# Seven block products for eight in seven W_up pairs of layer 1 of an encoder

## The chip, the core and the metric

The kernel runs on one core of one Trainium2 chip. The metric is the device time of one execution in microseconds (us), smaller is better. Five things work side by side on a core: TensorE (PE, matmuls, with its weight loads as PEld), VectorE (DVE), ScalarE (ACT), GpSimd (POOL) and SyncE (SP), which issues the DMAs. Each runs its own instructions in a fixed order; one that waits holds up all that stand behind it on its engine.

## What is computed

Two layers of an encoder over 512 positions of 1024 channels. The part that matters here is the second half of each layer:

```python
h = rmsnorm(x, norm2[l])
up = dwconv_centred(h @ w_up[l], conv_w[l], conv_b[l])   # 1024 -> 2 x 2816, then 3 taps along positions
gate, val = up[..., :D_FF], up[..., D_FF:]
x = x + (jax.nn.silu(gate) * val) @ w_down[l]            # 2816 -> 1024
```

Ahead of it each layer has a projection, a Fourier group, windowed attention and the output projection W_o, which the change does not touch.

## The kernel before

All activations are held transposed: channels on the 128 partitions, the 512 positions along the free axis. x is eight tiles x0 to x7 of 128x512, and h2[k] is the normed tile k, split into a high and a low part.

A product in float32 is made of three matmuls in fp32r (mm3): high by high (L120), low weights by high (L121), high weights by low (L122). So each weight has to be split: wsplit casts the high part on ACT (whi, L90) and subtracts for the low part on DVE (wlo, L93). whi and wlo have 5 buffers each of 512 columns; the raw weights (wraw) have 3 of 1024.

A pair fi of the FFN is a gate tile (column tile fi of W_up) and a value tile (fi + 22). There are 22 pairs in two halves (HALVES) of 11, each followed by its share of W_down. For each tile of a pair:

- one load of 512 KB on SP, two whi and two wlo (wchunks);
- 8 x 3 matmuls 128x512 into one bank of the rota FFN_BANKS;
- u, the bank times rb2 (the row factor of the norm, which is ready only after W_up has begun), on DVE (L93);
- the convolution: ACT with scale and bias into y, then two scalar-tensor-tensors on DVE, in place (L96).

Behind both tiles come Silu on ACT, the gate multiply (on POOL in layer 1, L93 POOL, on DVE in layer 0) and the split of the result into gu (ACT high, DVE low), which W_down reads. While layer 0 runs its FFN, weights of layer 1's first part are split ahead (presplit, `ahead`); in layer 1 nothing is.

PSUM has eight banks: three mm, two sc, two tp, one av. The tp banks serve transposes and the sums of the norms, and stand idle in the FFN of layer 1. A scheduler orders each engine's instructions by its own estimate of when they can start; the program's order is only where it begins, so instructions of neighbouring pairs are mixed on DVE and ACT.

## Time and profile before

| | |
|---|---|
| runs | 1056.22, 1057.18, 1057.36 us (median 1057.18) |
| the profiled execution | 1056.14 us |
| its span in the trace | 1054.3 us |
| mean granted TensorE clock | 0.999 |
| layer 1's W_up, first half | about 715 to 824 us of the span |

A row of the timeline gives the start and the length in us, the engine, the line, the operation and its tiles, a count where several follow one another, and in brackets the idle time ahead of it and what ended that. A row of a group gives busy us and the mean in ns of one, then the idle time ahead.

### The profile page before, as it was taken

The page shows a single profiled execution, that of the slowest core. Times are in us where ns is not written, and L with a number is a line of the kernel's source. Part 1 is how long each engine was busy: PE and PEld are TensorE (multiplying, and loading weights), DVE is VectorE, ACT ScalarE, POOL GpSimd, SP SyncE. Part 2 cuts the span into 40 slices and gives each one's busy share as a digit, 9 for nine tenths or more (in the row PEclk, how much of TensorE's full clock was granted, in tenths as well). Part 3 has the DMA queues.
Part 4 walks back from the last instruction along what each step waited for, and adds up shares of the span by engine and source line. Part 5 has one row for each costly group of instructions (what it writes and reads, how often), then busy time and mean ns, then how long its engine had stood idle before and what let it go on. Part 6 is the DMA issues. An engine that isn't in the chain of part 4 may idle for free.

```text
span 1054.3 us, 14425 instructions
## 1 busy us (share of the span) xinstructions
PE 1038.2 (98%) x5107; PEld 873.2 (83%) x5107; DVE 726.8 (69%) x1384; ACT 507.9 (48%) x939; POOL 90.8 (9%) x164
## 2 busy tenths in 40 slices
PE   8998999999999999999999999999999999999998
PEld 8986778888888888888899887888888888888887
DVE  8878768697767777777519775478877336878632
ACT  5339755455444445455423785246554224454421
POOL 0004410000000000000000152001101000101100
PEclk9999999999999999999999999999999999999999
DMA  7232152332269833239856313333332333332241
GB/s 273 83 115 87 58 193 81 100 100 96 78 226 353 324 100 101 89 114 322 280 181 221 113 62 99 122 100 94 101 101 74 96 115 100 98 101 82 82 150 48
DMA packets 60475, 140.03 MB, mean 133 GB/s; under 512 B 6642, under 2 KB 22258, under 8 KB 60404
## 3 DMA queue, kind: packets, MB, share of 16 engines
q1 hardware_dynamic: 60404, 139.12, 40.5%
q8 instruction: 40, 0.66, 0.3%
q14 instruction: 31, 0.25, 0.1%
HBM read 116.02 MB, written 23.07 MB: 132 GB/s over the span
## 4 chain that ended last, share of the span: by engine, by line
PE 93%; DVE 2%; DMA 2%; ACT 1%; issue 1%; POOL 0%; SPq 0%; ACTq 0%; DVEq 0%; POOLq 0%
PE ps L122 28%; PE ps L120 28%; PE ps L121 28%; PE ps L118 3%; PE ps L548 2%; PE ps L541 2%; PE ps L529 1%; DMA wraw<-in_w_qkv_dram 1%; PE ps L234 1%; PE ps L227 1%; ACT tA L90 0%; DMA x<-in_xT_dram 0%; DVE tA L533 0%; ACT act L90 0%; PE ps L500 0%
## 5 line engine op out<-in xcount | busy, mean ns | idle before, releaser
L90 ACT ACTIVATE whi<-wraw 128x512 fp32r<-128x512 f32 (+1 forms) x296 | 182.0, 616 | 290.8 <-PE ps L122 278.4
L120 PE MATMUL ps<-act,whi 128*128 128x512 f32 x768 | 298.9, 390 | 0.0
L121 PE MATMUL ps<-act,wlo 128*128 128x512 f32 x768 | 298.3, 389 | 0.0
L122 PE MATMUL ps<-act,whi 128*128 128x512 f32 x768 | 298.2, 389 | 0.0
L93 DVE TENSOR_TENSOR wlo<-wraw,whi 128x512 fp32r<-128x512 f32 (+1 forms) x304 | 219.7, 726 | 103.4 <-ACT whi L90 102.0
L122 PEld LDWEIGHTS ps<-act,whi 128*128 128x128 f32 x768 | 144.2, 188 | 30.1
L120 PEld LDWEIGHTS ps<-act,whi 128*128 128x128 f32 x768 | 144.2, 188 | 29.7
L121 PEld LDWEIGHTS ps<-act,wlo 128*128 128x128 f32 x768 | 144.2, 188 | 29.7
L96 DVE SCALAR_TENSOR_TENSOR tF<-tF,pb,tF 128x511 f32<-128x511 f32 x176 | 133.5, 763 | 11.1 <-ACT tF L90 8.7
L93 DVE TENSOR_TENSOR tF<-ps,rb 128x512 f32<-128x512 f32 x104 | 71.2, 689 | 77.9 <-PE ps L122 64.7
L120 PE MATMUL ps<-slab,whi 128*128 128x512 f32 (+2 forms) x212 | 82.2, 388 | 0.0
L122 PE MATMUL ps<-slab,whi 128*128 128x512 f32 (+2 forms) x212 | 79.9, 380 | 0.4 <-DVE slab L93 0.3
L121 PE MATMUL ps<-slab,wlo 128*128 128x512 f32 (+2 forms) x212 | 80.0, 378 | 0.0
L90 ACT ACTIVATE tF<-tF,pb 128x512 f32<-128x512 f32 x88 | 71.7, 816 | 11.3 <-DVE tF L93 4.6
L93 DVE TENSOR_TENSOR x<-x,ps 128x512 f32<-128x512 f32 (+1 forms) x49 | 32.9, 674 | 36.5 <-PE ps L122 36.3
L93 POOL TENSOR_TENSOR tF<-tF,tF 128x512 f32<-128x512 f32 x22 | 30.2, 1371 | 256.1 <-DVE tF L96 224.1
L120 PE MATMUL ps<-pT,whi 128*128 128x512 f32 (+1 forms) x132 | 50.5, 383 | 0.0
L121 PE MATMUL ps<-pT,wlo 128*128 128x512 f32 (+1 forms) x132 | 50.5, 383 | 0.0
L122 PE MATMUL ps<-pT,whi 128*128 128x512 f32 (+1 forms) x132 | 50.5, 383 | 0.0
L538 POOL TENSOR_SCALAR tA<-tA,den 128x256 f32<-128x256 f32 (+1 forms) x64 | 37.4, 590 | 145.1 <-DVE den L537 144.6
L533 DVE CUSTOM_DVE_ANT_0 tA<-ps,pb,nsink 128x256 f32<-128x256 f32 (+1 forms) x64 | 37.8, 603 | 14.5 <-PE ps L529 9.7
L122 PEld LDWEIGHTS ps<-slab,whi 128*128 128x128 f32 x212 | 39.7, 188 | 8.3 <-DVE slab L93 0.9
(178 smaller groups left out, 1485.0 us busy)
## 6 DMA issues: line engine op xcount, KB each, us to landing
wraw<-in_w_up_dram SPq DMA_DIRECT2D x88, 512.0 KB, 3.5
wraw<-in_w_down_dram SPq DMA_DIRECT2D x32, 512.0 KB, 3.7
kept<-tA SPq DMA_DIRECT2D x56, 256.0 KB, 5.7
whi<-kept SPq DMA_DIRECT2D x28, 256.0 KB, 3.0
wlo<-kept SPq DMA_DIRECT2D x28, 256.0 KB, 3.0
kept<-tA SPq DMA_DIRECT2D x32, 192.0 KB, 4.4
wraw<-in_w_down_dram SPq DMA_DIRECT2D x32, 192.0 KB, 2.4
wraw<-in_w_o_dram SPq DMA_DIRECT2D x8, 512.0 KB, 3.7
```

What stands on the lines that cost most here:

```text
L90: return nc.scalar.activation(out, in_, func, **kw)
L93: return (eng or nc.vector).tensor_tensor(out, a, b, op=op)
L96: return nc.vector.scalar_tensor_tensor(out=out, in0=a, scalar=s, in1=b, op0=op0, op1=op1)
L118: nc.tensor.matmul(out, a[0], b[0], start=start, stop=stop, **kw)
L120: nc.tensor.matmul(out, a[0], b[0], start=start, stop=False, **kw)
L121: nc.tensor.matmul(out, a[1], b[0], start=False, stop=False, **kw)
L122: nc.tensor.matmul(out, a[0], b[1], start=False, stop=stop, **kw)
L227: nc.tensor.matmul(pt[:, 2 * b:2 * b + 2], acc[:, b * P:(b + 1) * P], ones2, start=True, stop=True)
L533: nc.vector.tensor_tensor_reduce(out=pr[:, :n], in0=sc[:, :n], in1=mask[:, m0:m0 + n], scale=qs_scale[p][:, i, e:e + 1], scalar=nsink[:, l ...
L538: nc.gpsimd.tensor_scalar(pr[:, :n], pr[:, :n], den[:, i:i + 1], 1.0, op0=ALU.mult, op1=ALU.mult)
L541: tr = nc.tensor.transpose(pp[:, j * P:(j + 1) * P], pr[:, j * P:(j + 1) * P], ident)
L548: pv = nc.tensor.matmul(py[64 * e:64 * e + 64, i0 * P:(i1 + 1) * P], vp[:, j, 64 * g:64 * g + 64], pT[:, half, e, b0:b0 + 2 * (i1 - i0) + ...
```

## The change

In layer 1, the pairs 6, 8, 12, 14, 16, 18 and 20 are computed another way (up_seven); below they are the seven pairs, the others the eight pairs. The pair's two column tiles and the eight tiles of h are taken as a product of 2 x 2 blocks: a11 and a12 are the gate tile's weights for channels 0 to 511 and 512 to 1023, a21 and a22 the value tile's, and h is cut likewise into channels and into positions 0 to 255 and 256 to 511. Eight block products become seven, each of 4 x 3 matmuls 128x256, with sums of weights (s1 to s4, on DVE: s3 and s2 in a tile of their own, s1 in a21's place, s4 in a12's) and sums of h (T1 to T4). X and Y gather in the two tp banks, Z in a bank of the rota. X is copied by ACT after a11's product, goes on gathering, and is read three times more.

The sums of h are made once, by seven_h, behind each of the pairs 0 to 3: two ACT scalings, four half-wide DVE operations and two splits, into places that are free by then (h_rooms). And the gate multiply of layer 1 is on DVE now for all 22 pairs. The convolution is the same code in a function of its own; `pace`, and `acc` for layer 1, hold nothing that an instruction comes from.

```diff
--- before.py
+++ after.py
@@ -34,6 +34,8 @@
 FFN_BANKS = ("mm", "mm", "mm", "av", "sc", "sc")
 HALVES = [(0, 11), (11, 11)]
 
+SEVEN = ((), (6, 8, 12, 14, 16, 18, 20))
+
 def encoder_kernel(tc, t):
 
@@ -145,6 +147,8 @@
         return [wsplit(raw[:, c:min(c + step, n)], eng) for c in range(0, n, step)]
 
     kept = {}
+
+    pace = [None]
 
     def presplit(l):
 
@@ -371,6 +375,106 @@
         nc.sync.dma_start(raw.rearrange("p (k c) -> p k c", k=2),
                           t["w_in"][l, 2 * kk * P:2 * (kk + 1) * P, 0:FW].rearrange("(k p) c -> p k c", p=P))
         return [raw[:, k * 512:(k + 1) * 512] for k in range(2)]
+
+    LO, HI = slice(0, 256), slice(256, 512)
+
+    def sums_of_b(b1, b2):
+        t13, t24 = temp(512, "tF"), temp(512, "tF")
+        tt(t13[:, LO], b1[:, HI], b1[:, LO], ALU.subtract)
+        tt(t13[:, HI], b2[:, HI], b1[:, HI], ALU.subtract)
+        tt(t24[:, LO], t13[:, LO], b2[:, HI], ALU.subtract)
+        tt(t24[:, HI], t24[:, LO], b2[:, LO], ALU.add)
+        return t13, t24
+
+    def parts(g, src, keys, room):
+        two = [next(room), next(room)]
+        split(*two, src)
+        for key, cols in zip(keys, (LO, HI)):
+            g[key] = [z[:, cols] for z in two]
+
+    def h_rooms(l):
+
+        for tag in ("th0", "th1", "tl0", "tl1", "wt0", "wt1", "v", "accA", "accF", "acc"):
+            yield cp.tile([P, 512], F32R, tag=tag, name=nm("room"), bufs=1)
+        yield cp.tile([P, 512], F32R, tag="rb", name=nm("room"), bufs=2)
+        for _ in range(2):
+            yield tp.tile([P, 516], F32R, tag="tail", name=nm("room"), bufs=2)[:, :512]
+        for _ in range(2):
+            yield temp(512, "sq", F32R)
+        yield cp.tile([P, 512], F32R, tag="room", name=nm("room"), bufs=1)
+
+    def seven_h(k, l, h2, room):
+
+        b = [temp(512, "tF") for _ in range(2)]
+        for i in range(2):
+            act(b[i], x[k + 4 * i], scale=g2[:, l, k + 4 * i:k + 4 * i + 1])
+        g = dict(B11=[z[:, LO] for z in halves(h2[k])], B21=[z[:, LO] for z in halves(h2[k + 4])],
+                 B22=[z[:, HI] for z in halves(h2[k + 4])])
+        t13, t24 = sums_of_b(*b)
+        parts(g, t13, ("T1", "T3"), room)
+        parts(g, t24, ("T2", "T4"), room)
+        return g
+
+    def up_eight(l, fi, h2, ts, rb2):
+        for z in range(2):
+            w = wchunks(t["w_up"][l, fi + z * FT], 1024)
+            nps[0] += 1
+            o = psum(FFN_BANKS[nps[0] % len(FFN_BANKS)])
+            for k in range(KT):
+                mm3(o, [q[:, (k % 4) * P:(k % 4 + 1) * P] for q in w[k // 4]], [h2[k][:, s, :] for s in range(2)],
+                    k == 0, k == KT - 1)
+            u = temp(512, "tF")
+            tt(u, o, rb2, ALU.mult)
+            yield u
+
+    def up_seven(l, fi, h2, ts, rb2):
+        a, b = [wload(t["w_up"][l, fi + z * FT], 1024) for z in range(2)]
+        a11, a12, a21, a22 = a[:, :512], a[:, 512:], b[:, :512], b[:, 512:]
+        nps[0] += 1
+        X, Y, Z = [psum(tag)[:, LO] for tag in ("tp", "tp", FFN_BANKS[nps[0] % len(FFN_BANKS)])]
+        ua, ub = temp(512, "tF"), temp(512, "tF")
+
+        def product(o, w, key, start=False):
+            for k in range(4):
+                mm3(o, [z[:, k * P:(k + 1) * P] for z in w], ts[k][key], start and k == 0, k == 3, skip_group_check=True)
+
+        product(X, wsplit(a11), "B11", True)
+        act(ua[:, LO], X)
+        two = sp.tile([P, 1024], F32, tag="ropetab", name=nm("sums"), bufs=1)
+        s1, s2, s3, s4 = a21, two[:, :512], two[:, 512:], a12
+        tt(s3, a11, a21, ALU.subtract)
+        tt(s1, a21, a22, ALU.add)
+        product(Y, wsplit(s1), "T1", True)
+        act(ub[:, HI], Y)
+        product(Z, wsplit(a12), "B21", True)
+        tt(ua[:, LO], ua[:, LO], Z, ALU.add)
+        tt(s2, s3, a22, ALU.subtract)
+        product(X, wsplit(s2), "T2")
+        act(ua[:, HI], X)
+        tt(s4, a12, s2, ALU.add)
+        product(Y, wsplit(s4), "B22")
+        product(X, wsplit(s3), "T3")
+        tt(ub[:, HI], ub[:, HI], X, ALU.add)
+        tt(ua[:, HI], ua[:, HI], Y, ALU.add)
+        tt(ua, ua, rb2, ALU.mult)
+        yield ua
+        product(X, wsplit(a22), "T4")
+        tt(ub[:, LO], X, rb2[:, LO], ALU.mult)
+        tt(ub[:, HI], ub[:, HI], rb2[:, HI], ALU.mult)
+        yield ub
+
+    def conv(l, m, u):
+        y = temp(512, "tF")
+        pace[0] = act(y, u, AF.Identity, scale=cw[:, l, 1, m:m + 1], bias=cb[:, l, m:m + 1]).ins
+        stt(y[:, 1:], u[:, :-1], cw[:, l, 0, m:m + 1], y[:, 1:], ALU.mult, ALU.add)
+        stt(y[:, :-1], u[:, 1:], cw[:, l, 2, m:m + 1], y[:, :-1], ALU.mult, ALU.add)
+        return y
 
     acc = accum()
     xg = [norm_tile(k, g1[:, 0, :], acc) for k in range(KT)]
@@ -698,34 +802,24 @@
         rb2 = row_rstd(col_rstd(acc2, 1.0 / D))
 
-        acc = accum()
+        acc = accum() if l == 0 else None
         if l == 0:
             tabs, alts, wt = load_tables(1)
         ahead = presplit(l + 1) if l < L - 1 else iter(lambda: 0, 1)
+        room, ts = h_rooms(l), []
         for f0, nf in HALVES:
             gu = []
             for fi in range(f0, f0 + nf):
                 ys_ = []
                 n = fi - f0
-                for z in range(2):
-                    m = fi + z * FT
-                    w = wchunks(t["w_up"][l, m], 1024)
-                    nps[0] += 1
-                    o = psum(FFN_BANKS[nps[0] % len(FFN_BANKS)])
-                    for k in range(KT):
-                        mm3(o, [q[:, (k % 4) * P:(k % 4 + 1) * P] for q in w[k // 4]], [h2[k][:, s, :] for s in range(2)],
-                            k == 0, k == KT - 1)
-                    u = temp(512, "tF")
-                    tt(u, o, rb2, ALU.mult)
-                    y = temp(512, "tF")
-                    act(y, u, AF.Identity, scale=cw[:, l, 1, m:m + 1], bias=cb[:, l, m:m + 1])
-                    stt(y[:, 1:], u[:, :-1], cw[:, l, 0, m:m + 1], y[:, 1:], ALU.mult, ALU.add)
-                    stt(y[:, :-1], u[:, 1:], cw[:, l, 2, m:m + 1], y[:, :-1], ALU.mult, ALU.add)
-                    ys_.append(y)
+                for z, u in enumerate((up_seven if fi in SEVEN[l] else up_eight)(l, fi, h2, ts, rb2)):
+                    ys_.append(conv(l, fi + z * FT, u))
                     if (2 * n + z) % 3 == 2:
                         next(ahead)
+                if SEVEN[l] and len(ts) < 4:
+                    ts.append(seven_h(len(ts), l, h2, room))
                 act(ys_[0], ys_[0], AF.Silu)
-                tt(ys_[0], ys_[0], ys_[1], ALU.mult, nc.gpsimd if l else nc.vector)
+                tt(ys_[0], ys_[0], ys_[1], ALU.mult)
                 if n < 4:
                     a = pair("slab")
                 elif n < 8:
```

Up to W_up of layer 1 the engines' orders are the same in both kernels. The first place is on PE where pair 6 begins. Before, its gate tile (ps_1677) ends and the value tile (ps_1685) follows at once, 24 wide matmuls each:

```order
L120 MATMUL ps_1677_7557<-act_1563_7003,whi_1675_7553 128x512
L121 MATMUL ps_1677_7557<-act_1563_7003,wlo_1676_7554 128x512
L122 MATMUL ps_1677_7557<-act_1563_7003,whi_1675_7553 128x512
L120 MATMUL ps_1685_7598<-act_1524_6827,whi_1681_7590 128x512
L121 MATMUL ps_1685_7598<-act_1524_6827,wlo_1682_7591 128x512
L122 MATMUL ps_1685_7598<-act_1524_6827,whi_1681_7590 128x512
L120 MATMUL ps_1685_7598<-act_1527_6847,whi_1681_7590 128x512
L121 MATMUL ps_1685_7598<-act_1527_6847,wlo_1682_7591 128x512
```

Now three products of pair 6 stand there, X = ps_1705, Y = ps_1706, Z = ps_1707, 36 narrow matmuls in all. Then comes pair 7's gate tile (ps_1733), an eight pair; its weights are whi_1729 and wlo_1730, then whi_1731 and wlo_1732. Here Z ends and pair 7 begins:

```order
L123 MATMUL ps_1707_7624<-act_1563_7003,wlo_1716_7665 128x256
L124 MATMUL ps_1707_7624<-act_1563_7003,whi_1715_7664 128x256
L122 MATMUL ps_1733_7776<-act_1524_6827,whi_1729_7768 128x512
L123 MATMUL ps_1733_7776<-act_1524_6827,wlo_1730_7769 128x512
L124 MATMUL ps_1733_7776<-act_1524_6827,whi_1729_7768 128x512
L122 MATMUL ps_1733_7776<-act_1527_6847,whi_1729_7768 128x512
```

And a little later, X's third product stands between the first matmul with whi_1731 and the one with wlo_1732:

```order
L123 MATMUL ps_1733_7776<-act_1539_6899,wlo_1730_7769 128x512
L124 MATMUL ps_1733_7776<-act_1539_6899,whi_1729_7768 128x512
L122 MATMUL ps_1733_7776<-act_1547_6929,whi_1731_7772 128x512
L122 MATMUL ps_1705_7622<-room_1592_7121,whi_1717_7682 128x256
L123 MATMUL ps_1705_7622<-room_1592_7121,wlo_1718_7683 128x256
L124 MATMUL ps_1705_7622<-room_1593_7122,whi_1717_7682 128x256
L122 MATMUL ps_1705_7622<-room_1617_7226,whi_1717_7682 128x256
```

The second place is DVE where it makes the low parts of pair 7's gate tile. Before, these are wlo_1691 and wlo_1693, with a u, a convolution and a split between them in a steady pattern:

```order
L93 TENSOR_TENSOR tF_1670_7537<-ps_1669_7512,rb_1569_7023 128x512
L93 TENSOR_TENSOR wlo_1691_7637<-wraw_1689_7634,whi_1690_7636 128x512
L96 SCALAR_TENSOR_TENSOR tF_1671_7539<-tF_1670_7537,pb_96,tF_1671_7539 128x511 x2
L93 TENSOR_TENSOR wlo_1693_7641<-wraw_1689_7634,whi_1692_7640 128x512
L93 TENSOR_TENSOR tF_1678_7582<-ps_1677_7557,rb_1569_7023 128x512
L93 TENSOR_TENSOR pT_1655_7458<-tF_1663_7498,pT_1655_7458 128x512
L93 TENSOR_TENSOR wlo_1699_7678<-wraw_1697_7675,whi_1698_7677 128x512
```

Now wlo_1730 stands behind pair 6's last low part (wlo_1725), and wlo_1732 behind the u and the convolutions of pairs 4 and 5:

```order
L95 TENSOR_TENSOR wlo_1725_7740<-wraw_1704_7620,whi_1724_7739 128x512
L95 TENSOR_TENSOR wlo_1730_7769<-wraw_1728_7766,whi_1729_7768 128x512
L95 TENSOR_TENSOR tF_1693_7567<-ps_1692_7542,rb_1569_7023 128x512
L98 SCALAR_TENSOR_TENSOR tF_1685_7523<-tF_1684_7521,pb_96,tF_1685_7523 128x511
L98 SCALAR_TENSOR_TENSOR tF_1677_7482<-tF_1676_7480,pb_96,tF_1677_7482 128x511
L98 SCALAR_TENSOR_TENSOR tF_1685_7523<-tF_1684_7521,pb_96,tF_1685_7523 128x511
L98 SCALAR_TENSOR_TENSOR tF_1694_7569<-tF_1693_7567,pb_96,tF_1694_7569 128x511
L95 TENSOR_TENSOR tF_1701_7608<-ps_1700_7583,rb_1569_7023 128x512
L95 TENSOR_TENSOR tF_1677_7482<-tF_1677_7482,tF_1685_7523 128x512
L98 SCALAR_TENSOR_TENSOR tF_1694_7569<-tF_1693_7567,pb_96,tF_1694_7569 128x511
L98 SCALAR_TENSOR_TENSOR tF_1702_7610<-tF_1701_7608,pb_96,tF_1702_7610 128x511
L95 TENSOR_TENSOR wlo_1732_7773<-wraw_1728_7766,whi_1731_7772 128x512
```

What moved: the two low parts, which had one convolution between them, have nine rows between them, two of them u of pair 5 (tF_1693 and tF_1701).

ACT has this at the same place; whi_1729 and whi_1731 are the high parts of pair 7's gate tile, tF_1708 the copy of X of pair 6 (it reads ps_1705):

```order
L92 ACTIVATE whi_1724_7739<-wraw_1704_7620 128x512
L92 ACTIVATE whi_1729_7768<-wraw_1728_7766 128x512
L92 ACTIVATE tF_1685_7523<-tF_1684_7521,pb_96 128x512
L92 ACTIVATE tF_1694_7569<-tF_1693_7567,pb_96 128x512
L92 ACTIVATE tF_1677_7482<-tF_1677_7482 128x512
L92 ACTIVATE tF_1702_7610<-tF_1701_7608,pb_96 128x512
L92 ACTIVATE whi_1731_7772<-wraw_1728_7766 128x512
L92 ACTIVATE pT_1686_7529<-tF_1677_7482 128x512
L92 ACTIVATE tF_1708_7625<-ps_1705_7622 128x256
```

The second cast of pair 7's weights has come to stand behind the convolution that reads tF_1701.

The third place is DVE behind pair 6's last product (ps_1705 by rb is its half of the value tile); ps_1733 and ps_1741 are pair 7's tiles, wlo_1761, wlo_1763 and wlo_1766 low parts of pair 8, and wlo_1771 is the first low part of pair 9, the next eight pair:

```order
L95 TENSOR_TENSOR tF_1709_7626<-ps_1705_7622,rb_1569_7023 128x256
L95 TENSOR_TENSOR tF_1734_7801<-ps_1733_7776,rb_1569_7023 128x512
L95 TENSOR_TENSOR wlo_1761_7935<-wraw_1744_7852,whi_1760_7934 128x512
L95 TENSOR_TENSOR tF_1742_7842<-ps_1741_7817,rb_1569_7023 128x512
L98 SCALAR_TENSOR_TENSOR tF_1726_7757<-tF_1709_7626,pb_96,tF_1726_7757 128x511
L98 SCALAR_TENSOR_TENSOR tF_1735_7803<-tF_1734_7801,pb_96,tF_1735_7803 128x511
L95 TENSOR_TENSOR wlo_1763_7951<-sums_1753_7878,whi_1762_7950 128x512
L98 SCALAR_TENSOR_TENSOR tF_1726_7757<-tF_1709_7626,pb_96,tF_1726_7757 128x511
L95 TENSOR_TENSOR wlo_1766_7974<-wraw_1745_7854,whi_1765_7973 128x512
L98 SCALAR_TENSOR_TENSOR tF_1735_7803<-tF_1734_7801,pb_96,tF_1735_7803 128x511
L95 TENSOR_TENSOR wlo_1771_8003<-wraw_1769_8000,whi_1770_8002 128x512
```

Before, DVE did there what the steady pattern above shows for every pair; now the low parts of pair 8 and the convolutions of pairs 6 and 7 stand ahead of pair 9's first.

## The prediction

> **What bounds the kernel now.** First the page's busy shares and chain of waits, then the windows of layer 1's W_up (columns: window, then busy us and count on PE, PEld, DVE, ACT, POOL; granted clock, DMA share, GB/s).
>
> ```profile
> PE 1038.2 (98%) x5107; PEld 873.2 (83%) x5107; DVE 726.8 (69%) x1384; ACT 507.9 (48%) x939; POOL 90.8 (9%) x164
> PE 93%; DVE 2%; DMA 2%; ACT 1%; issue 1%; POOL 0%; SPq 0%; ACTq 0%; DVEq 0%; POOLq 0%
> 715.00:735.00 20.00, 20.00 (x91) 16.54 (x90) 19.21 (x29) 14.31 (x21) 3.15 (x3) 1.00 0.25 79
> 735.00:757.00 22.00, 22.00 (x99) 18.22 (x98) 19.22 (x26) 12.00 (x19) 4.29 (x3) 1.00 0.33 100
> 757.00:779.00 22.00, 22.00 (x99) 18.22 (x98) 17.45 (x23) 11.11 (x17) 2.57 (x2) 1.00 0.30 97
> ```
>
> PE has no gap in this stage and holds 93% of the chain. So PE time removed is time won, as long as the others keep PE fed. DVE has the least room: 17.45 of 22 us for two pairs in the steady stretch, 19.2 of 20 and of 22 before it.
>
> **PE: what is removed.** The cost of a matmul is the step from start to start: 512 wide from the first two rows, 256 wide (the halved last W_down) from the next two.
>
> ```profile
> 1034.83 0.39 PE L120 MATMUL ps<-m,whi 128*128 128x512 f32 x1
> ...
> 1042.76 0.39 PE L122 MATMUL ps<-m,whi 128*128 128x512 f32 x1
> 1042.98 0.28 PE L120 MATMUL ps<-slab,whi 128*128 128x256 f32 x1
> ...
> 1050.78 0.28 PE L122 MATMUL ps<-m,whi 128*128 128x256 f32 x1
> L122 PEld LDWEIGHTS ps<-act,whi 128*128 128x128 f32 x768 | 144.2, 188 | 30.1
> ```
>
> 35 steps take 7.93 us, so 0.2266 each; 65 steps take 7.80, so 0.120 each. The narrow step is more than half, because part of a step does not shrink. A pair goes from 48 × 0.2266 = 10.88 to 84 × 0.120 = 10.08 us: 0.80 less, not an eighth. **Seven pairs: −5.6 us**, all there is to win. A weight load takes 0.188 us, longer than a narrow step, but in the tail the loads overlapped and the 0.120 held with new weights for each matmul.
>
> The Trainium skill ("TensorE: Matmul & The Clock Gate", section "Back-to-back issue gap") speaks against the change: it gives a sustained 131 ns at 512 columns and 81 at 128; my estimate between them is 98 at 256, by which a pair would go from 6.3 to 8.2 us and the seven lose 13. The trace disagrees at 512 columns (0.2266), so the sum stands on the rows.
>
> **DVE: what is added.** Times of DVE instructions, by start in the timeline, then groups.
>
> ```profile
> 715.79 1.29 DVE L93 TENSOR_TENSOR tF<-ps,rb 128x512 f32<-128x512 f32 x2 [1.98 <-ACT rb L90]
> 717.00 0.68 DVE L93 TENSOR_TENSOR wlo<-wraw,whi 128x512 fp32r<-128x512 f32 x1
> 717.60 0.68 DVE L93 TENSOR_TENSOR tF<-ps,rb 128x512 f32<-128x512 f32 x1
> 718.20 3.39 DVE L96 SCALAR_TENSOR_TENSOR tF<-tF,pb,tF 128x511 f32<-128x511 f32 x5
> 721.50 0.69 DVE L93 TENSOR_TENSOR wlo<-wraw,whi 128x512 fp32r<-128x512 f32 x1
> ...
> 730.43 1.40 DVE L96 SCALAR_TENSOR_TENSOR tF<-tF,pb,tF 128x511 f32<-128x511 f32 x2
> ...
> 744.85 0.68 DVE L93 TENSOR_TENSOR wlo<-wraw,whi 128x512 fp32r<-128x512 f32 x1
> 746.02 0.69 DVE L93 TENSOR_TENSOR tF<-ps,rb 128x512 f32<-128x512 f32 x1 [0.50 <-PE ps L122]
> ...
> 753.28 1.53 DVE L96 SCALAR_TENSOR_TENSOR tF<-tF,pb,tF 128x511 f32<-128x511 f32 x2
> ...
> 756.90 0.69 DVE L93 TENSOR_TENSOR tF<-ps,rb 128x512 f32<-128x512 f32 x1 [1.36 <-PE ps L122]
> ...
> 760.29 1.74 DVE L93 TENSOR_TENSOR wlo<-wraw,whi 128x512 fp32r<-128x512 f32 x1 [0.27 <-ACT whi L90]
> ```
> ```profile
> 760.19 1.29 POOL L93 TENSOR_TENSOR tF<-tF,tF 128x512 f32<-128x512 f32 x1 [9.59 <-DVE tF L96]
> ```
> ```profile
> L93 DVE TENSOR_TENSOR tF<-tF 128x255 f32<-128x255 f32 x16 | 6.1, 417 | 0.0
> L90 ACT ACTIVATE pT<-ps 128x256 f32<-128x256 f32 x32 | 12.1, 378 | 7.7 <-PE ps L541 7.3
> ```
>
> Back to back, a tensor-tensor (TT) starts 0.60 after the last (717.00, 717.60, 718.20) and a scalar-tensor-tensor (STT) 0.66 ((721.50 − 718.20)/5). A half TT is bounded by half of 0.60 and its duration 0.417; I take 0.335, its duration less the same 0.08 overlap. Two STTs where one reads the other take 1.53 for 1.40.
>
> An eight-product pair with the gate multiply on DVE has 8 TT + 4 STT = 7.44 us. A seven-product pair has 14 TT (7 low parts, 4 weight sums, u, gate, its low part), 5 halves and 4 STT = 12.7 us. Together 20.2 in a cycle of 10.88 + 10.08 = 20.96 on PE. It fits with 0.8 to spare. The gate on DVE costs 0.60 a pair, and what it takes away is the block at 760.29, where a low part took 1.74 for 0.69 beside POOL's multiply at 760.19: 1.05 a pair. ACT gets 3 casts and 3 half copies (0.378) more per seven pair, about 3 us, beside 11.11 of 22 busy. SP issues the same two loads per pair.
>
> **h's sums take the catching up.** Before, DVE enters W_up late (1.98 us waiting for rb at 715.79), runs without a gap until 744.85 and first waits for PE at 746.02. seven_h adds 4 halves and 2 TT, 2.54 us, to each of the first four pairs; 7.44 + 2.54 = 10.0 in 10.88 leaves hardly any catching up. **Stall A: pair 7 behind pair 6.** PE reaches pair 6 where it does now:
>
> ```profile
> 756.71 0.39 PE L120 MATMUL ps<-act,whi 128*128 128x512 f32 x1
> ```
>
> After three products (36 × 0.120) the next matmul but one, at 761.26, needs wlo_1730. On DVE 48 TT, 17 STT and 16 halves stand between the first u at 715.79 and it: 28.8 + 11.2 + 5.4 = 45.4, so it starts at 761.2 if DVE never waits and ends at 761.9. Walking these rows against ACT's, with the table load below ahead of the first Silu, I find 1.7 us of waiting on DVE (0.4 there, 0.9 for a cast of s2 that waits for a free whi buffer, 0.4 in two more): it ends at 763.5, **2.3 us late**.
>
> ```profile
> 720.34 1.28 ACT L90 ACT_TABLE_LOAD   x1 [0.69 <-DVE tF L96]
> ...
> 722.17 0.62 ACT L90 ACTIVATE whi<-wraw 128x512 fp32r<-128x512 f32 x1
> 722.88 0.82 ACT L90 ACTIVATE tF<-tF,pb 128x512 f32<-128x512 f32 x1
> ```
>
> Then ACT: whi_1731, the second cast of pair 7's gate tile, is queued behind the conv of tF_1701, which DVE computes after wlo_1730, a u and four STTs. From wlo_1730's start at 762.8: 0.60 + 0.60 + 4 × 0.66 + 0.69 + 0.72 (conv, by its step) + 0.62 gives 768.8. PE, moved by 2.3, has work until 766.0: **2.8 more**. X's third product then waits for ACT's copy of X, behind the pT cast: 0.54 + 0.38 after whi_1731, PE having one matmul meanwhile: **0.5**. Stall A is 5.6. If DVE never waited it would be 3.2: the second low part ends at 768.2 + 0.2 against 765.4, plus 0.2 of the copy. If ACT and DVE were always ahead it would be nothing.
>
> **Stall B: pair 9 behind pair 8.** When pair 6's last product ends, DVE has, in this order, a half, u, lo, u, STT, STT, lo, STT, lo, STT (0.335 + 5 × 0.60 + 4 × 0.66 = 6.0) and then wlo_1771, 0.69, after a handover of 0.2: 6.9 us. PE has three products of pair 8 and one matmul: 4.3 + 0.2 = 4.5. **2.3 us**, whatever went before. If the u rows were ready early, it would be nothing.
>
> **Second half.** After W_down DVE is ahead. ACT's chain in pairs 16, 18 and 20 (cast of s3, conv, cast of a22, Silu, copy of X) ends about 0.25 late by the casts and convs above: **0.8** in all, between 0 and 2. W_down's starts are covered: the last gate halves are split before the 20 us of matmuls ahead of them run out.
>
> **Sum.** −5.6 + 5.6 + 2.3 + 0.8 = +3.1 on the profiled execution's 1056.14: 1059.2. That execution is the lowest beside runs of 1056.22, 1057.18 and 1057.36, so I add half of the 1.04 to their median: **1059.7**.
>
> **Rivals.**
> - *The operands come in time* (faster). If DVE comes to wlo_1730 before 760.6, 2.2 us earlier than walked, and B's u rows early, nothing is left but −5.6 + 0.8: 1051.3. For it: the gate's block goes, and the cycle fits by 0.8. Against it: the sum without any wait already ends after 761.26.
> - *Shorter stalls* (no change). A at its bound of 3.2 and B at 2.3: +0.7, 1056.8 to 1057.5. It decides if DVE's and ACT's waits fall on each other.
> - *DVE becomes the bound* (slower). Its sums read what it has just written; if some 8 neighbours of a cycle pay the 0.13 of the 753.28 row, a cycle is 21.2 against 20.96, and A grows by 2 us or so: with five cycles about +6.4, 1062.5. By full durations (0.68, 0.417, 0.75) a cycle is 23.1 and the second half alone loses up to 10, but the rows at 717.00 to 718.20 speak against that.
> - *Weight loads bind.* 84 × 0.188 = 15.8 a pair would give +35. The tail's rows exclude it as far as they go.
>
> The Trainium skill ("VectorE: DVE Perf Modes", section "The DRAIN you can't avoid") says that the next operation does not start until the pipe is empty; by that, DVE would be the bound, as in the third rival's full durations. The trace has starts 0.60 apart at 0.68 long and disagrees for these.
>
> **How the numbers follow.** Forecast with both stalls 0.40 (1058.5 to 1060.7); in time 0.20; shorter stalls 0.25; DVE-bound 0.13; loads 0.02. A measurement of this kernel tells about 0.2%, 2.1 us, from no change: 1055.1 to 1059.3 counts as same. Faster: 0.20 and 0.06 of the shorter stalls, 0.26. Same: 0.19 of these and 0.13 of the forecast's lower part, 0.32. Slower: the rest, 0.42. The range reaches from 1051.5 (half of the fast case) to 1064.
>
> **What would show it.** PE's steps of 0.120 in the seven pairs; a gap on PE ahead of pair 7's second matmul (about 2.3, released by DVE's wlo), one at its second cast (2.8, by ACT's whi), one of 2.3 at pair 9's; DVE without idle time from 716 to 768; none of PE's gaps over 0.5 after pair 11. No gap at pairs 7 and 9 would make the prediction wrong, and so would gaps in every cycle of the second half.

## The result and the profile after

The changed kernel took 1062.85 us (median of 4 runs, 1060.94 to 1062.94), the kernel before 1056.97 beside it (4 runs, 1056.22 to 1057.36). The ratio is 1.0052, with a 95% interval of 1.0040 to 1.0064: slower by 5.9 us, where 2.5 were forecast. Its profiled execution has a span of 1060.6 us. One of the ten executions of run e3 below took 1734.51 us at a granted clock of 0.556; its ratio leaves that one out.

From the page of the changed kernel: busy shares and the chain of waits.

```profile
PE 1037.2 (98%) x5359; PEld 882.5 (83%) x5359; DVE 759.1 (72%) x1507; ACT 529.1 (50%) x997; POOL 61.8 (6%) x142
PE 90%; DVE 5%; ACT 3%; issue 1%; DMA 1%; POOL 0%; SPq 0%; ACTq 0%; DVEq 0%; POOLq 0%
```

PE is on the chain for 90% instead of 93%; DVE and ACT have taken its place. The windows of W_up in layer 1 say where (columns as before the change: busy time of PE, PEld, DVE, ACT and POOL, then the granted clock):

```profile
735.00:757.00 22.00, 22.00 (x98) 18.21 (x97) 21.25 (x39) 14.41 (x23) 0.00 (x0) 1.00 0.23 72
757.00:779.00 22.00, 17.41 (x100) 15.00 (x99) 20.39 (x35) 11.82 (x21) 0.00 (x0) 0.92 0.24 73
779.00:801.00 22.00, 20.04 (x123) 17.68 (x122) 19.46 (x33) 12.64 (x22) 0.00 (x0) 1.00 0.31 96
```

Before, PE had no gap in this stretch. Now it is idle for 4.6 us in one window and 2.0 in the next, and in the first of them the granted clock is 0.92. PE's timeline of the changed kernel has every gap; ahead of each of them stands the last matmul before it:

```profile
757.93 0.28 PE L122 MATMUL ps<-act,whi 128*128 128x256 f32 x1
...
762.10 0.28 PE L124 MATMUL ps<-act,whi 128*128 128x256 f32 x1
763.10 0.50 PE L122 MATMUL ps<-act,whi 128*128 128x512 f32 x1 [0.72 <-ACT whi L92]
764.70 0.50 PE L123 MATMUL ps<-act,wlo 128*128 128x512 f32 x1 [1.10 <-DVE wlo L95]
...
767.11 0.39 PE L124 MATMUL ps<-act,whi 128*128 128x512 f32 x1
769.98 0.50 PE L122 MATMUL ps<-act,whi 128*128 128x512 f32 x1 [2.48 <-ACT whi L92]
770.76 0.47 PE L122 MATMUL ps<-room,whi 128*128 128x256 f32 x1 [0.28 <-ACT tF L92]
...
773.17 0.41 PE L124 MATMUL ps<-room,whi 128*128 128x256 f32 x1
773.38 0.63 PE L123 MATMUL ps<-act,wlo 128*128 128x512 f32 x1
773.81 0.63 PE L124 MATMUL ps<-act,whi 128*128 128x512 f32 x1
774.23 0.44 PE L122 MATMUL ps<-act,whi 128*128 128x512 f32 x1
...
790.29 0.28 PE L124 MATMUL ps<-sq,whi 128*128 128x256 f32 x1
791.29 0.50 PE L122 MATMUL ps<-act,whi 128*128 128x512 f32 x1 [0.72 <-ACT whi L92]
793.03 0.50 PE L123 MATMUL ps<-act,wlo 128*128 128x512 f32 x1 [1.24 <-DVE wlo L95]
```

A pause is the step from start to start less the usual 0.227 (wide) or 0.120 (narrow). At pair 7: 0.88, 1.37, 2.64 and 0.55 us, 5.44 in all. At pair 9: 0.88 and 1.51, together 2.39. The rows from 770.76 to 773.38 show something else: eleven narrow steps and the one behind them take 2.62 us, 0.218 each in place of 0.120, and the wide steps up to 774.23 are 0.43 and 0.42. PE waits for nothing there; it runs at half speed.

For the comparison of runs, one clock is used: the start of the first matmul after the row factor (716.10 in the changed kernel, 714.88 before) begins the FFN of layer 1, the first matmul on W_down ends W_up's first half, and the last matmul of all ends the FFN. The rows that bound these parts, of the kernel before and then of the changed one:

```profile
714.88 0.48 PE L122 MATMUL ps<-act,whi 128*128 128x512 f32 x1
811.11 0.39 PE L120 MATMUL ps<-slab,whi 128*128 128x512 f32 x1
870.95 0.39 PE L120 MATMUL ps<-act,whi 128*128 128x512 f32 x1
990.62 0.39 PE L120 MATMUL ps<-slab,whi 128*128 128x512 f32 x1
```
```profile
716.10 0.48 PE L124 MATMUL ps<-act,whi 128*128 128x512 f32 x1
820.48 0.39 PE L122 MATMUL ps<-slab,whi 128*128 128x512 f32 x1
880.32 0.39 PE L122 MATMUL ps<-act,whi 128*128 128x512 f32 x1
996.91 0.39 PE L122 MATMUL ps<-slab,whi 128*128 128x512 f32 x1
1057.06 0.28 PE L124 MATMUL ps<-m,whi 128*128 128x256 f32 x1
```

The first half went from 96.23 to 104.38 us, the second from 119.67 to 116.59; the whole FFN from 335.90 (to 1050.78) to 340.96: 5.06 longer. The remaining 1.22 us lie ahead of the FFN, where both kernels run the same instructions. Windows near the start of the two profiled executions, of the kernel before and of the changed one, have the reason:

```profile
26.50:30.00 3.50, 3.09 (x20) 3.09 (x21) 0.00 (x0) 3.09 (x9) 0.36 (x1) 1.00 0.20 76
```
```profile
26.50:30.00 3.50, 3.44 (x14) 3.44 (x15) 0.34 (x1) 3.09 (x9) 0.00 (x1) 0.54 0.12 44
```

In the changed kernel's profile PE ran these 3.5 us at a granted clock of 0.54. That happened in 10 of this study's 14 profiles and not in the others (the run with pairs 6 and 8 alone has 1.00), so it belongs to the execution and not to the change: the FFN begins at 714.60 to 714.95 us in the four profiles without it, and at 715.96 us or later in those with it. It is also why the FFN's own length is the better measure below.

### The profile page after: what moved, and what is told of

It is laid out like the page before. It is cut to its first block, busy times and chain, and to the rows that moved or that the text cites. A ratio compares the mean times of both kernels' runs of the same rounds, so it can differ in the third digit from the quotient of the medians.

```text
span 1060.6 us, 15111 instructions
## 1 busy us (share of the span) xinstructions
PE 1037.2 (98%) x5359; PEld 882.5 (83%) x5359; DVE 759.1 (72%) x1507; ACT 529.1 (50%) x997; POOL 61.8 (6%) x142
## 4 chain that ended last, share of the span: by engine, by line
PE 90%; DVE 5%; ACT 3%; issue 1%; DMA 1%; POOL 0%; SPq 0%; ACTq 0%; DVEq 0%; POOLq 0%
PE ps L124 27%; PE ps L122 27%; PE ps L123 27%; PE ps L120 3%; PE ps L652 2%; PE ps L645 1%; PE ps L633 1%; DVE tF L98 1%; DVE wlo L95 1%; PE ps L238 1%; ACT tA L92 1%; PE ps L231 1%; ACT tF L92 1%; DVE tF L95 0%; DVE act L98 0%
## 5 line engine op out<-in xcount | busy, mean ns | idle before, releaser
L92 ACT ACTIVATE whi<-wraw 128x512 fp32r<-128x512 f32 (+1 forms) x303 | 186.0, 616 | 288.4 <-PE ps L124 259.8
L122 PE MATMUL ps<-act,whi 128*128 128x512 f32 (+1 forms) x740 | 278.6, 378 | 3.9 <-ACT whi L92 3.9
L123 PE MATMUL ps<-act,wlo 128*128 128x512 f32 (+1 forms) x740 | 279.2, 378 | 2.3 <-DVE wlo L95 2.3
L95 DVE TENSOR_TENSOR wlo<-wraw,whi 128x512 fp32r<-128x512 f32 (+1 forms) x311 | 206.4, 667 | 103.7 <-ACT whi L92 102.2
L124 PE MATMUL ps<-act,whi 128*128 128x512 f32 (+1 forms) x740 | 278.8, 378 | 0.0
L122 PEld LDWEIGHTS ps<-act,whi 128*128 128x128 f32 x740 | 139.2, 188 | 30.2 <-ACT whi L92 4.7
L123 PEld LDWEIGHTS ps<-act,wlo 128*128 128x128 f32 x740 | 139.4, 188 | 28.5 <-DVE wlo L95 3.0
L124 PEld LDWEIGHTS ps<-act,whi 128*128 128x128 f32 x740 | 139.4, 188 | 25.0
L98 DVE SCALAR_TENSOR_TENSOR tF<-tF,pb,tF 128x511 f32<-128x511 f32 x176 | 129.6, 747 | 7.0 <-ACT tF L92 5.7
L95 DVE TENSOR_TENSOR tF<-ps,rb 128x512 f32<-128x512 f32 (+1 forms) x97 | 64.0, 668 | 53.6 <-PE ps L124 40.4
L124 PEld LDWEIGHTS ps<-slab,whi 128*128 128x128 f32 x212 | 39.7, 188 | 8.2 <-DVE slab L95 0.9
L122 PEld LDWEIGHTS ps<-slab,whi 128*128 128x128 f32 x212 | 39.9, 188 | 7.4 <-issue 0.8
```

Source lines behind the costliest of these rows:

```text
L92: return nc.scalar.activation(out, in_, func, **kw)
L95: return (eng or nc.vector).tensor_tensor(out, a, b, op=op)
L98: return nc.vector.scalar_tensor_tensor(out=out, in0=a, scalar=s, in1=b, op0=op0, op1=op1)
L122: nc.tensor.matmul(out, a[0], b[0], start=start, stop=False, **kw)
L123: nc.tensor.matmul(out, a[1], b[0], start=False, stop=False, **kw)
L124: nc.tensor.matmul(out, a[0], b[1], start=False, stop=stop, **kw)
```

## The experiments

The theory: the loss is two stalls of PE, at the eight pairs behind the first two seven pairs, because DVE and ACT are late; the h sums make DVE late; the second half is a gain. The rivals: DVE is the bound in every cycle; the order on PE, ACT or DVE makes the stalls whatever the load; the cost lies elsewhere. Times are medians, and beside the experiments the kernel before took 1057.2 to 1057.6 on the same chip; FFN lengths are from the profile of each run, as above.

| run | time, us | ratio and interval | first half | second half | FFN |
|---|---|---|---|---|---|
| before | 1056.97 | | 96.23 | 119.67 | 335.90 |
| changed | 1062.85 | 1.0052 (1.0040 to 1.0064) | 104.38 | 116.59 | 340.96 |
| e1 second half alone | 1053.80 | 0.9967 (0.9957 to 0.9978) | 96.23 | 116.61 | 332.83 |
| e2 first half alone | 1065.54 | 1.0075 (1.0060 to 1.0090) | 104.36 | 119.69 | 344.03 |
| e3 no half sums of h | 1055.86 | 0.9981 (0.9971 to 0.9990) | 97.70 | 116.58 | 334.28 |
| e4 gate on POOL | 1064.38 | 1.0069 (1.0053 to 1.0086) | 103.43 | 119.42 | 342.85 |
| f1 pair 8, not 6 | 1055.26 | 0.9977 (0.9968 to 0.9986) | 96.97 | 116.60 | 333.57 |
| f2 other seven pairs | 1059.67 | 1.0018 (1.0009 to 1.0027) | | | 338.00 |
| f3 filled pause | 1063.05 | 1.0048 (1.0035 to 1.0062) | 104.97 | 116.60 | 341.56 |
| f4 six buffers, no half sums | 1062.53, one run | | 96.81 | 120.19 | 338.44 |
| g1 eight pairs and a rule | 1055.96 | 0.9980 (0.9971 to 0.9989) | | | 334.61 |
| g2 changed, with the rule | 1065.06 | 1.0070 (1.0056 to 1.0083) | 107.04 | 116.61 | 343.64 |
| g3 other seven, with the rule | 1054.69 | 0.9969 (0.9955 to 0.9983) | | | 333.33 |
| h1 pair 10 and second half | 1053.66 | 0.9964 (0.9950 to 0.9977) | | | 332.02 |

Where halves are blank, the last products of a pair and the first of W_down are mixed on PE.

### e1 and e2: one half each

```diff
-SEVEN = ((), (6, 8, 12, 14, 16, 18, 20))
+SEVEN = ((), (12, 14, 16, 18, 20))      # e1
+SEVEN = ((), (6, 8))                    # e2
```

> Only pairs 12, 14, 16, 18 and 20 have seven products; h's sums stay behind pairs 0 to 3 and the gate multiply on DVE. Theory (the loss is two stalls of PE in the first half, at the low parts and casts of the eight pair behind a seven pair; h's sums and the gate multiply cost nothing by themselves): W_up's first half takes 96.2 us as before, the second half 116.6 as in the changed kernel, so 3.1 us less than before, about 1053.9. Rival (h's sums load DVE and ACT so that PE waits even without seven pairs): the first half is longer by 2 us or more and the time is 1056 or above.

> Only pairs 6 and 8 have seven products. Theory: the first half keeps its stalls (104.4 us for 96.2 before), the second half is 119.7 as before: about 8.2 us over before, 1065. Rival (the loss depends on the whole set, or lies elsewhere): less than 4 us over before.

Both came out as the theory has it: with the second half alone the first half of W_up takes 96.23 us, to the hundredth what it took before, though h's sums and the gate multiply are there. So these cost PE nothing by themselves. With pairs 6 and 8 alone, the loss is all in the first half (104.36), and e2's pauses are those of the changed kernel. Five seven pairs in the second half give 3.1 us; two in the first take 8.1.

### e3: no backlog from h's sums

```diff
-        t13, t24 = sums_of_b(*b)
+        t13, t24 = b
```

> The four half-wide DVE operations of each of h's sums are left out (16 in all, about 5.4 us of DVE ahead of pair 7), so that T1 to T4 hold the scaled h itself and the seven pairs compute something else; every matmul stays. Theory (a backlog of DVE, made by h's sums, is what makes pair 7 late): the stall of 5.4 us at pair 7 falls to under 1 us, and with it the stretch at half clock behind it, about 1.5 us; the stall of 2.4 at pair 9 stays: about 1056.5. Rival (the order alone makes pair 7 wait: its second cast stands behind the convolution of pair 5 on ACT, whatever the backlog): at least 2.7 us of the stall stay and the time is 1059 or above.

The first half fell from 104.38 to 97.70 us. PE's waits of this run at pair 7, and then two others alike at pair 9:

```profile
763.43 0.50 PE L122 MATMUL ps<-act,whi 128*128 128x512 f32 x1 [0.72 <-ACT whi L92]
764.22 0.39 PE L122 MATMUL ps<-room,whi 128*128 128x256 f32 x1 [0.29 <-ACT tF L92]
```

In place of 5.44 and 2.39 there are 1.44 and 1.44 us, and the waits for DVE's low parts and the half clock are gone. That the backlog is gone shows in DVE's multiply for pair 5's second tile, here in e3 and then in the changed kernel; PE ends that tile near 758 in both:

```profile
758.68 0.68 DVE L95 TENSOR_TENSOR tF<-ps,rb 128x512 f32<-128x512 f32 x1
```
```profile
767.81 0.68 DVE L95 TENSOR_TENSOR tF<-ps,rb 128x512 f32<-128x512 f32 x1
```

But the scheduler also chose another order in e3: X's third product stands behind one matmul of pair 7 and not behind thirteen, and on ACT pair 5's last convolution stands ahead of pair 7's first cast and not between its two casts. The first low part of pair 7 comes hardly earlier (47.4 us after the FFN's beginning, 47.9 in the changed kernel); PE needs it later. So h's sums, with the order that they bring, were worth 4.0 us at pair 7, 0.95 at pair 9 and the stretch at half clock; the load alone was not separated from the order by this run. Two points missed: at pair 7 more than 1 us stayed, and pair 9 gained although it was expected not to. What stays is the same at both: 0.88 us for a cast and 0.56 for the copy of X. That is what this order costs without a backlog; g2 below has nearly the same order on PE with the backlog.

### e4: the gate multiply on POOL

```diff
-                tt(ys_[0], ys_[0], ys_[1], ALU.mult)
+                tt(ys_[0], ys_[0], ys_[1], ALU.mult, nc.gpsimd if l else nc.vector)
```

> The gate multiply of layer 1 is on POOL again, all else as changed. By the prediction's terms DVE loses 0.60 us of work a pair and gets back a block of 1.05 us: 0.45 worse a pair, 2.7 us by pair 7, so that the stall there grows by up to 2.7 us and the time to 1064 to 1066. Rival (the block falls where DVE waits anyway): DVE is 3.6 us earlier at pair 7 and the time is about 1059.

The time is in the expected range but not for the expected reason: the first half is 0.95 us shorter than in the changed kernel, and the second 2.83 longer. The pauses at pair 7 shrank from 5.44 to 3.20 us, and a second fall of the clock, at pair 9, took back 1.6. In the second half PE waited at three seven pairs for ACT's copy of X, as in this row:

```profile
916.76 0.38 PE L122 MATMUL ps<-room,whi 128*128 128x256 f32 x1 [1.23 <-ACT tF L92]
```

So the gate multiply on DVE is worth 2.8 us in the second half; why the copy is late there was not followed further. The size of "1.05 a pair" at pair 7 was not borne out.

### f1: pair 8 first

```diff
-SEVEN = ((), (6, 8, 12, 14, 16, 18, 20))
+SEVEN = ((), (8, 12, 14, 16, 18, 20))
```

> Pair 6 has eight products again; pairs 8, 12, 14, 16, 18 and 20 have seven. Theory (the stall at the first seven pair is DVE's backlog from h's sums, which four eight pairs of 7.4 us in 10.9 clear by pair 8): at pair 9 only what was left without a backlog stays, about 1.4 us, no stretch at half clock, so W_up's first half takes 96.2 - 0.8 + 1.4 = 96.9 us and the time is about 1054.5. Rival (a first seven pair in the first half costs its 5 to 7 us wherever it stands): 1058 or above.

The first half is 96.97 us, 0.07 from the expected 96.9. PE's only waits there are 0.88 and 0.56 at pair 9. Two eight pairs more between h's sums and the first seven pair are enough to clear DVE's backlog: DVE takes pair 9's first low part at 785.54, when its cast ends (784.87 + 0.63). The pair still loses: it gains 0.8 and costs 1.44.

### f2: the odd pairs of the second half

```diff
-SEVEN = ((), (6, 8, 12, 14, 16, 18, 20))
+SEVEN = ((), (10, 11, 13, 15, 17, 19, 21))
```

> Seven pairs again, but others: 10, 11, 13, 15, 17, 19 and 21, so that pair 10 and pair 21 are followed by W_down and not by an eight pair. Theory (place and backlog are what matters, and W_down's weights do not wait): the first half takes 96.2 - 0.8 = 95.4 us, the second 119.7 - 6 x 0.8 + 1 = 115.9, the time is about 1052.6. Rival (whatever stands behind a seven pair waits 1.4 us or more, W_down too): 1055 or above.

This missed by 7 us, and W_down waited as well, as the rival has it. From pair 13 on the same two waits come at every seven pair, five times, the last of them at W_down's first matmul behind pair 21. Here is the first:

```profile
895.00 0.28 PE L124 MATMUL ps<-act,whi 128*128 128x256 f32 x1
896.00 0.50 PE L122 MATMUL ps<-act,whi 128*128 128x512 f32 x1 [0.72 <-ACT whi L92]
896.79 0.39 PE L122 MATMUL ps<-room,whi 128*128 128x256 f32 x1 [0.29 <-ACT tF L92]
```

One wide matmul of the next eight pair stands here between Z's last matmul and X's third product. Its weights need the whi buffer that Z's weights leave, since the eight pair's first cast is the eighth, counted from a11's, and there are five buffers; so the cast begins only when Z ends. Behind that cast on ACT stands the copy of X for which the third product waits. In the changed kernel's second half this same matmul stands behind X's third product (at pairs 12 and 14 behind Y's second too), 1.44 us later or more, and there is no wait for a cast. 5 x 1.44 = 7.2 of loss against 7 x 0.8 of gain is 1.6; the FFN is 2.1 longer.

### f4: another buffer

```diff
-"tA": (512, 6)
+"tA": (512, 4)
...
-        hi = wp.tile([P, 512], F32R, tag="whi", name=nm("whi"), bufs=5)
-        lo = wp.tile([P, 512], F32R, tag="wlo", name=nm("wlo"), bufs=5)
+        hi = wp.tile([P, 512], F32R, tag="whi", name=nm("whi"), bufs=6)
+        lo = wp.tile([P, 512], F32R, tag="wlo", name=nm("wlo"), bufs=6)
...
-        t13, t24 = sums_of_b(*b)
+        t13, t24 = b
```

> The kernel without the four half-wide operations in each of h's sums (T1 to T4 hold the scaled h), with 6 instead of 5 buffers for whi and wlo; the room comes from tA, 4 buffers for 6, which changes the parts ahead of the FFN, so only the FFN is compared. Theory (the 0.9 us by which an eight pair's first cast is late is the wait for a whi buffer that pair 6's Z frees just ahead of it): both waits of 0.9 at pairs 7 and 9 go, and the first half takes 97.7 - 1.8 = 95.9 us or less. Rival (the cast is late because of ACT's queue): the waits stay within 0.2.

PE waits for no cast in this run, at pair 7, at pair 9 or later, which is what the theory of the buffer says. But the scheduler orders DVE otherwise too, and PE now waits 1.7 us for a low part at pair 9, and in the second half 1.1 to 1.4 for low parts at three pairs and 1.4 for a copy of X. So the first half is 96.81, not 95.9. The buffer is one cause of the 0.88, as far as a run with another order can show it; a sixth alone wins nothing.

### f3: the pause filled

```diff
+                if (l, fi, z, k) == (1, 7, 0, 4):
+                    spare = psum(FFN_BANKS[(nps[0] + 1) % len(FFN_BANKS)])
+                    for _ in range(10):
+                        with tc.issue_after(last):
+                            last = nc.tensor.matmul(spare, h2[0][:, 0, :P], h2[0][:, 0, :], start=True, stop=True).ins
...
```

> The changed kernel with ten 128x512 matmuls of no use (2.27 us) in PE's order ahead of the matmul of pair 7 that waited 2.6 us for the second cast. Theory (that pause is what lets the granted clock fall to a half for some 4 us behind it): the pause shrinks to under 0.5, the clock stays at 1.00, X's third product takes 0.12 a matmul and the first half shrinks from 104.4 by 1.6 to 1.9 us; the time is about 1061. Rival (the half clock has another cause, or a slow stretch of the pace is due to the operands): the half clock stays, or the time does not fall.

The ten matmuls filled the third pause, X's third product ran at 0.12 behind them, and the first half is 104.97, 0.6 longer than without them: the half clock came earlier, behind the first two pauses, as the windows of this run show (granted clock in the third column from the end).

```profile
762.00:764.70 2.70, 0.88 (x5) 0.36 (x4) 2.70 (x6) 1.70 (x3) 0.00 (x0) 1.00 0.37 152
764.70:768.50 3.80, 3.80 (x10) 2.98 (x11) 3.80 (x7) 1.45 (x2) 0.00 (x0) 0.55 0.48 138
768.50:773.00 4.50, 4.50 (x27) 3.96 (x26) 4.50 (x8) 2.92 (x7) 0.00 (x0) 1.00 0.20 38
```

Pauses of 0.88 and 1.37 us were enough here, and the same two were not in the changed kernel's profile. And at pair 9, behind the pauses of 0.88 and 1.52, the clock fell a second time: nine wide steps take 795.97 − 792.33 = 3.64 us for 2.04 of work, 1.6 that the changed kernel does not lose behind the same pauses. So a fall does not need the 2.6 us pause. At pair 7 it came in every run that has the backlog there (the changed kernel, e2, e4, f3, g2) and in none without (e1, e3, f1); at pair 9 in e4 and f3 alone. The last section says what goes with it.

### g1, g2, g3: a rule for one matmul

The first matmul of an eight pair behind a seven pair may not stand ahead of X's third product (`after` is an argument of mm3 already):

```diff
-        product(X, wsplit(s2), "T2")
+        third[0] = product(X, wsplit(s2), "T2")
...
-                    k == 0, k == KT - 1)
+                    k == 0, k == KT - 1, third[0] if z == k == 0 else None)
+            third[0] = None
```

> The changed kernel, pairs as they are, with the same rule. Theory: at pairs 7 and 9 the 1.44 us that come from the order go, DVE's backlog stays: the first half shrinks from 104.4 us by 2.9 to 101.5, or to under 100 if the granted clock keeps up too; the time is about 1058 to 1060. Rival (the low parts are late by the backlog whatever stands on PE): the first half stays above 103.

> The seven pairs 10, 11, 13, 15, 17, 19 and 21 with the same rule. Theory: the five waits of 0.9 and the five of 0.6 go, the FFN shrinks from 338.0 to about 331 us, and the time from 1059.7 to about 1052.6. Rival (the operands would come late behind X's third product too): over 335.

> Eight seven pairs, 8, 10, 11, 13, 15, 17, 19 and 21, and one rule more: the first matmul of an eight pair behind a seven pair may not stand ahead of X's third product on PE. Theory (what is left without a backlog, 0.9 + 0.6 us at each of them, comes from that one matmul, whose cast needs the buffer that Z has just freed, and from X's copy, which stands behind that cast on ACT): no wait of PE for a cast is left, the FFN of layer 1 takes 335.9 - 8 x 0.8 + about 1 = 330.5 us, 5.4 less than before, and the time is about 1052. Rival (the operands would come late behind X's third product too): waits of 0.5 us or more at five or more pairs, the FFN 333 us or more.

In g2 the first half grew to 107.04 us, against the expectation: the pauses at pair 7 moved to one place, and at pair 9 2.15 us for a copy of X are there instead of 2.39. PE's rows at pair 7:

```profile
761.97 0.28 PE L124 MATMUL ps<-act,whi 128*128 128x256 f32 x1
...
770.11 0.58 PE L122 MATMUL ps<-room,whi 128*128 128x256 f32 x1 [7.86 <-ACT tF L92]
```

X's third product waits 8.0 us for ACT's copy of X, which stands behind convolutions that wait for DVE. With a backlog the rule takes from PE the work that it did meanwhile. Beside e3, where X's third product stands behind Z and one matmul more and waits 1.44 us in all with the cast, this shows the load: nearly the same order on PE costs 8.0 with the backlog. In g3, without one, it does what it should at four places of five; at pair 13, 1.67 us for the copy stay. The FFN shrank from 338.00 to 333.33, where 331 was expected. In g1 the same 1.67 came at pairs 8 and 13, and the FFN is 334.61; of the expected 330.5 it misses 3.3 by these two waits and 0.8 by short ones. An eighth pair won nothing over seven.

### h1: the lowest

```diff
-SEVEN = ((), (6, 8, 12, 14, 16, 18, 20))
+SEVEN = ((), (10, 12, 14, 16, 18, 20))
```

> Pairs 10, 12, 14, 16, 18 and 20 have seven products, in the scheduler's own order. Theory (a seven pair that W_down follows gives its 0.8 us without a wait, the even pairs of the second half lose about 1 us in all): the FFN of layer 1 takes 335.9 - 0.8 - 3.1 = 332.0 us and the time is about 1053, the lowest of these kernels. Rival (pair 10 waits for its own operands, or W_down for the last gate values behind it): 333 us or more, and no better than without pair 10 (1053.8).

The FFN takes 332.02 us, as expected. This kernel is faster than both kernels of the change: 0.9964 of the one before. Against e1 (1053.80) its 0.8 us show in the FFN and are below what the times can tell.

## Why the prediction was right, point by point

The direction was right and the time lies in the range; the loss was forecast as 2.5 us and measured as 5.9. The range, 1051.5 to 1064, holds gains and losses alike, so the time alone says little for the prediction; the stalls, forecast one by one, say more.

- *−5.6 us for seven pairs.* It holds: narrow matmuls run at 0.120 (757.93 and on), and the second half, with five, gives 3.08 of 4.0.
- *Stall A, 5.6 us.* Measured 5.44: 2.25 ahead of pair 7's second matmul (2.3 forecast), 2.64 at its second cast (2.8), 0.55 at the copy of X (0.5). DVE and ACT show the walk. In these rows the second of the two low parts is wlo_1730; ACT's is first the convolution of pair 5, then the second cast, pT and the copy:

```profile
763.36 1.28 DVE L95 TENSOR_TENSOR wlo<-wraw,whi 128x512 fp32r<-128x512 f32 x2
```
```profile
768.59 0.81 ACT L92 ACTIVATE tF<-tF,pb 128x512 f32<-128x512 f32 x1 [1.35 <-DVE tF L95]
769.31 0.61 ACT L92 ACTIVATE whi<-wraw 128x512 fp32r<-128x512 f32 x1
769.83 0.61 ACT L92 ACTIVATE pT<-tF 128x512 fp32r<-128x512 f32 x1
770.35 0.36 ACT L92 ACTIVATE tF<-ps 128x256 f32<-128x256 f32 x1
```

  wlo_1730 begins at 763.36 + 0.60 = 763.96 by the step of 0.60. Less the 1.22 us by which this FFN began later, that is 762.7; forecast 762.8. The cast ends at 769.92, or 768.7 less 1.22; forecast 768.8 (the terms given there add up to 768.7). DVE's waits from the first u on are 1.20 us (0.27, 0.75, 0.18) for a walked 1.7. One thing was not seen: the first 0.88 of the 2.25 are a wait for the cast, which needs the buffer that Z frees; DVE's low part came later still and so set the sum.
- *Stall B, 2.3 us.* Measured 2.39, and DVE's list took the time that was counted: from the half multiply (the first of two operations in the first row) to the end of the first low part of pair 9 it is 792.98 − 786.31 = 6.7 us, forecast 6.7 without the handover. The first 0.88 is again a wait for the cast, covered by the low part.

```profile
786.31 1.02 DVE L95 TENSOR_TENSOR tF<-ps,rb 128x256 f32<-128x256 f32 x2
792.30 0.68 DVE L95 TENSOR_TENSOR wlo<-wraw,whi 128x512 fp32r<-128x512 f32 x1
```

  "Whatever went before" was wrong: in e3, without the backlog and in another order, DVE's part of it is gone and 1.44 of another kind stays.
- *Second half, 0.8 us lost.* Measured 4.0 − 3.08 = 0.9, and for the reason given: at pairs 16, 18 and 20 X's third product begins some 0.2 us late, when ACT's copy of X ends behind casts, a convolution and Silu. Here are the copy and the matmul at pair 16:

```profile
937.21 0.36 ACT L92 ACTIVATE tF<-ps 128x256 f32<-128x256 f32 x1
937.62 0.38 PE L122 MATMUL ps<-room,whi 128*128 128x256 f32 x1
```

- *The step that failed* is the sum, which had no term for the granted clock. Behind the pauses at pair 7 PE ran at half speed; the rows give 773.38 − 770.76 = 2.62 for 1.44 us of work, and 0.85 for 0.45 in the two wide steps behind: 1.6 us. With it, −5.6 + 5.44 + 2.39 + 0.9 + 1.6 = 4.7 for the 5.06 of the FFN; the last 0.3 were not traced. In the two profiled executions 1.22 us more lie ahead of the FFN, by the clock near the start; how much of this is in the 5.9 between the medians is not known.
- *The rivals.* DVE was not the bound: no gap stands in each cycle of the second half. That this rival's number, 1062.5, lies next to the measured 1062.85 is chance. Operands in time was what happened with the first seven pair placed later (e1, h1), and gave 3.1 to 3.9 us there.
- *The rule on DVE's pipe* from the Trainium skill ("VectorE: DVE Perf Modes", "The DRAIN you can't avoid") would have had operations start one length apart, save those for which the section itself allows an earlier start; in the changed kernel two take 1.28 us, 0.60 and 0.68, so the rows decided rightly.

## What to carry to other kernels

Fewer operations on the bounding engine gain nothing where the engines that feed it are still behind from another step: count their backlog at the place where the new form begins, from the last time at which they waited for nothing. Look then at the order: one matmul that needs a buffer which the instruction ahead of it frees, put ahead of work that needs no such wait, cost 1.44 us each time, more than the 0.8 that the change wins in a pair. A fixed order moves the wait and does not remove it while the operand is late (g2). And pauses that left PE less than half busy in one window of 3.41 us cost some 1.6 us on top (last section).

## What the runs showed of the hardware

The granted clock falls to a half after pauses that are short. These windows are of the changed kernel, around the fall at pair 7:

```profile
762.00:767.00 5.00, 3.18 (x15) 2.27 (x14) 5.00 (x9) 2.96 (x5) 0.00 (x0) 1.00 0.52 176
767.00:770.00 3.00, 0.52 (x4) 0.10 (x2) 3.00 (x6) 1.65 (x4) 0.00 (x0) 1.00 0.02 7
770.00:774.20 4.20, 3.92 (x15) 3.44 (x16) 3.21 (x6) 2.08 (x6) 0.00 (x0) 0.61 0.46 127
```

The longest pause there is 2.64 us, and in f3 two of 0.88 and 1.37 were followed by 3.8 us at 0.55. The Trainium skill ("TensorE: Matmul & The Clock Gate", "HAM oscillation — how this bites in real kernels") gives as its rule "no PE-idle gaps >~3.4µs"; here shorter ones did it.

The traces show what goes with a fall. Read in slices of half a us, with the clock taken as full or half at each moment (PE's wide steps are 0.227 or 0.427 us), the granted clock gives each fall's beginning and end. Up to 1050 us every fall lasts 3.41 or 3.42 us, and the one around g2's pause of 8.0 lasts 10.24, three times as long. In one execution the falls stand on a grid. From the end of the fall near the start to the end of the one at pair 7 it is 744.11 us in the changed kernel, 744.10 in g2, 740.69 in e4 and 737.27 in f3: 218.00, 218.00, 217.00 and 216.00 times 3.4133. From pair 7's to pair 9's it is 27.31 us in f3 (8.00 times) and 23.90 in e4 (7.00). So time is cut into windows of 3.41 us that do not begin anew with a pause. The page's account of a window of 3413 ns that runs freely ("What's actually happening") agrees with this grid.

PE's busy share of a window goes with the clock of the next:

| run and place | window from, us | PE's busy share | clock in the next |
|---|---|---|---|
| changed, pair 7 | 760.68 | 0.65 | 1.00 |
| changed, pair 7 | 764.09 | 0.82 | 1.00 |
| changed, pair 7 | 767.50 | 0.19 | 0.50 |
| changed, pair 9 | 791.40 | 0.64 | 1.00 |
| f3, pair 7 | 761.65 | 0.47 | 0.50 |
| f3, pair 9 | 788.95 | 0.42 | 0.50 |
| e4, pair 7 | 763.39 | 0.44 | 0.50 |
| e4, pair 9 | 787.28 | 0.48 | 0.50 |
| g2, pair 9 | 791.63 | 0.51 | 1.00 |
| g3, pair 13 | 896.66 | 0.56 | 1.00 |

In the eleven profiles in which a fall gives the grid, every window between 700 and 1040 us with a share of 0.48 or less was followed by one at half clock, and every one with 0.51 or more by one at full clock. So the same pauses brought a fall in one execution and none in another: in f3 those at pair 7 lie in one window, in the changed kernel they are split between two. The border is not sharp everywhere, and the busy times of matmuls are modelled: near the start, where PE runs other matmuls, a window with a share of 0.56 (e4) was followed by a fall.
